# A hybrid attention layer: bias rows in key order, weight loads and norm steps put at other places of the program

## The chip, the core and the metric

One core of a Trainium2 chip runs the whole layer as one program. The metric is the device time of that program in microseconds; the median of three runs of the kernel before is 1379.38 us (1378.87 to 1380.16). Lower is better.

## What is computed

One encoder layer over 16 meta tokens and 1024 tokens of width 1024. After an RMS norm, one input projection yields the latents of group A (multi-head latent attention, 8 heads, dense), q, k and v of group B (neighbourhood attention, 16 heads of 64) and the gates of both groups. The core of group B:

```
s_win  = einsum(q_row, k_win) * scale + rel_bias[:, dr_idx, dc_idx]   # 8 rows x 16 columns of the 16 x 64 grid
s_meta = einsum(q_row, k_meta) * scale + meta_bias                    # 16 meta tokens: keys for every query
p      = softmax(concat(s_win, s_meta))
out    = p_win @ v_win + p_meta @ v_meta
```

Both groups' outputs are multiplied by SiLU of their gates, concatenated, projected by w_out and added to the input. Everything is float32; products are kept precise by splitting an operand into a high part (float32r) and a low part (the difference) and multiplying hi x hi, hi x lo and lo x hi.

## The kernel before

The stages, in the order of the program: (1) 0 to 83 us: the norm and the first two groups of gate columns. (2) 83 to 198 us: gate groups 2 to 5, each 384 columns (group 5: 128), as blocks of 128 columns by two halves of 512 tokens; one such gate is 24 matmuls. (3) 198 to 712 us: group B in 8 pairs of heads. (4) to 760 us: the latents. (5) to 1206 us: group A. (6) the output projection.

**Weights.** `w_split` (L139) loads a quarter of a weight block (two of the eight 128-row chunks) by a DMA on SP's queue into `wnf` (two buffers), ScalarE casts the high part `wnh`, and VectorE or GpSimd (`engs`) subtracts to get the low part `wnl`. `wnh` and `wnl` have six slots in pool `wp`; the last quarter (`own=wx`) has two slots `wnhx`, `wnlx` in a pool of its own, opened at L365 on memory which the setup used before.

**Bias.** In gate group 3, `bias_rows` (L377) makes 16 times two matmuls, and VectorE writes `base`, 24 column offsets by 16 key rows for each head. In groups 4 and 5, `stage_bias` (L390) has GpSimd lay out, for a pair of heads, three forms of the bias (800 values a partition for inner query tiles with the column mask added, 272 each for the first and the last tile) and sends them to `bias_d` in DRAM. `na_bias` (L454) loads the three forms of a pair.

**Group B's loop (L691).** Step g works on four query tiles at once: the projection of tile pr = g + 6 (t = pr mod 8 within pair p), scores `na_qk` of tile g + 1, transposes of the probabilities `na_ptr` of tile g, and probabilities times v `na_pv` of tile g - 1. TensorE's order is exactly the program's (`manual_schedule` for PE only); projections are cut into three parts with the other matmuls between them. All other engines' orders come from a planner, which places an instruction where its own model of the run finds its inputs and buffers ready and the engine free, and among several ready ones takes the one that stands earlier in the program. On the chip each engine then runs its list strictly in order. Parts of a step that the change touches: `na_load(p+1, t-2)` at the start of steps t = 2 to 5 (the weight splits of the next pair), `na_acc` (evictions of the projection: squares, raw q and k, `v_split`), `na_norm` in odd steps (sum, a power on GpSimd in `rstd` at L95, three small VectorE steps, one product), `na_meta` at t = 1 (16 matmuls for the meta tokens, at the end of the step, then their norm), `na_sum`/`na_fin` (reciprocals and gate product of four tiles) and `lat_nat` (the latents' norm, six tiles of it in the loop's last steps).

Of the kernel before, what the change touches and what calls it, by code (L numbers as in the profile page):

```python
# [10 lines left out]
F32 = mybir.dt.float32  # L11
F32R = mybir.dt.float32r
AF = mybir.ActivationFunctionType
ALU = mybir.AluOpType
# [20 lines left out]
WB = WI + 2 * WE  # L35
# [14 lines left out]
def hybrid_layer(ctx, tc, x, x_t, meta, meta_t, norm_w, w_na, w_g, w_lat, lat_w, w_uq, w_ukv, vec128, qpe_w, kpe_w,  # L50
# [27 lines left out]
    bias_d = dram.tile([NPAIR, P, 2, WB], F32, name="bias_d")  # L78
# [4 lines left out]

    def rstd(ss, n, cnt, np_=P, E=G):
# [3 lines left out]
        t = small.tile([P, n], F32, name="rs_t", tag=f"rs_t{n}")[:np_]  # L88

# [5 lines left out]
        G.tensor_tensor(y, v, mhalf[:np_, :n], op=ALU.pow)  # L95
        E.tensor_tensor(t, y, y, op=ALU.mult)
# [6 lines left out]
        return y  # L103

# [238 lines left out]
    base = sp1.tile([P, 16, NB, ROWS], F32, name="base")  # L343
# [40 lines left out]
    sg = sctx.enter_context(tc.tile_pool(name="stg", bufs=1))  # L384

    imask = load(c_imask, [P, WI], "imask", sp1)
    metab = load_bc(meta_bias, 16 * NM, "metab", sp1).rearrange("p (h m) -> p h m", h=16)
    G.tensor_scalar(metab, metab, -1.0, None, op0=ALU.mult)

    def stage_bias(p):  # L390

        E = G
        bs = base[:, 2 * p:2 * p + 2].rearrange("p h b r -> p h (b r)")
        bo = sg.tile([P, 2, WB], F32, name="sgb", bufs=3)
        bi, b0, b7 = bo[:, :, :WI], bo[:, :, WI:WI + WE], bo[:, :, WI + WE:]
        mb = metab[:, 2 * p:2 * p + 2, :]
        im = imask[:, None, :].to_broadcast([P, 2, WI])
        for o, bb, w in ((0, 0, 128), (144, 8, 128), (288, 16, 112)):
            E.tensor_tensor(bi[:, :, o:o + w], bs[:, :, bb * 16:bb * 16 + w], im[:, :, o:o + w], op=ALU.add)
        E.memset(bi[:, :, 128:144], MASK)  # L400
        E.tensor_copy(bi[:, :, 272:288], mb)
        for b_, c in ((b0, 128), (b7, 0)):
            E.tensor_copy(b_[:, :, 0:128], bs[:, :, c:c + 128])
            E.tensor_copy(b_[:, :, 128:144], mb)
            E.tensor_copy(b_[:, :, 144:272], bs[:, :, c + 128:c + 256])
        G.dma_start(bias_d[p], bo)

    todo_b = list(range(NPAIR))
    for gr in range(2, 6):
        gw = g_load(gr, (G, G) if gr < 4 else (V, V))  # L410
        for b in range(min(3, 16 - 3 * gr)):
            for hf in (1, 0):
# [6 lines left out]
                elif gr > 3 and todo_b:  # L419
                    stage_bias(todo_b.pop(0))  # L420
    sctx.close()
# [22 lines left out]
    st = {}  # L444

    def na_load(p, k):
        if k == 0:
            st[p] = {"w": []}
        d = st[p]
        d["w"].append(w_split(w_na[p, :, 2 * k:2 * k + 2, :], 384, (V, V), parts=True, own=wx if k == 3 else None))  # L450
        if k == 3:
            d["w"] = w_views(d["w"])

    def na_bias(p):  # L454
        c = 0
        for name, w, n in (("bi", WI, 2), ("b0", WE, 1), ("b7", WE, 1)):
            t = st[p][name] = np2.tile([P, 2, w], F32, name=name, bufs=n)
            nc.sync.dma_start(t, bias_d[p, :, :, c:c + w])
            c += w
# [7 lines left out]
    def na_nat(src, n, width):  # L467

        sq = np2.tile([P, 512], F32, name="sqn")[:n, :width]
        raw = np2.tile([P, P], F32, name="natm", bufs=1)[:n, :width]  # L470
        S.activation(sq, src, AF.Square)
        S.copy(raw, src)
        return na_norm(sq, raw, n, width)

    def na_norm(sq, raw, n, width):
# [3 lines left out]
        r = rstd(ss, g, 1.0 / 64, n, V)  # L479
        r3 = raw.rearrange("p (g d) -> p g d", g=g)  # L480
        V.tensor_tensor(r3, r3, r[:, :, None].to_broadcast([n, g, 64]), op=ALU.mult)
        return raw
# [17 lines left out]
    def na_meta(p):  # L500
        d = st[p]
        acc = bank("s")
        proj(acc[:, :256], NT, d["w"], 128, 384)
        kv = np2.tile([P, 256], F32, name="kvm", bufs=1)[:NM]
        meta_sum(kv, acc[:, :256])
        Vm = VM[p % 2]
        v_split(Vm, kv[:, 128:256], NM)
        d["Vm"] = Vm
        d["natm"] = na_nat(kv[:, :128], NM, 128)
# [7 lines left out]
    def na_acc(p, t, acc):  # L517
# [13 lines left out]
        d["V"][t] = vt  # L531

# [28 lines left out]
    def na_qk(p, t):  # L561
# [7 lines left out]
        for j in range(2):  # L569
# [7 lines left out]
                                   op0=ALU.add, op1=ALU.min, accum_out=mn)  # L577
            S.activation(sb, sb, AF.Exp, scale=-1.0, bias=mn, accum_out=d["sum", t // 4][:, t % 4, j:j + 1])  # L578
            d["p", t, j] = sb

    def na_ptr(p, t, j):

        d = st[p]
        sb = d["p", t, j]
# [44 lines left out]
    def na_sum(p, hf):  # L629
# [9 lines left out]
               r.rearrange("p t j -> p (t j)")[:, :, None].to_broadcast([P, 8, 64]))  # L639
        ps = bank("tr")  # L640
# [47 lines left out]
    for k in range(4):  # L688
        na_load(0, k)
# [625 lines left out]
```

## Time and profile before

| | us |
|---|---|
| median of three runs | 1379.38 |
| profiled execution | 1379.65 |
| its span in the profile | 1377.8 |
| TensorE busy | 1316.7 (96%) |
| VectorE busy | 958.1 (70%) |
| ScalarE busy | 809.8 (59%) |
| GpSimd busy | 436.4 (32%) |

The profiled execution is 1.85 us longer than its span, which begins with the first and ends with the last recorded instruction. A busy TensorE can run at either of two clocks, 1.2 or 2.4 GHz; the granted clock is given as a share of 2.4 GHz. "PE" is matmuls, "PEld" the loading of their weights, DVE is VectorE, ACT ScalarE, POOL GpSimd, SPq the queue on which SP issues DMAs.

### The profile page before, as it was taken

How to read it: one execution, taken by the hardware profiler on the slowest of the kernel's cores; microseconds unless marked ns; L12 is line 12 of the kernel's file. 1: busy time of each engine (PE TensorE's matmuls, PEld its weight loads, DVE VectorE, ACT ScalarE, POOL GpSimd, SP SyncE). 2: the span in 40 equal slices, each digit the busy share in tenths (PEclk: the TensorE clock that was granted, in tenths of full speed). 3: DMA queues.
4: the chain of work that ended last, by engine and by line, in shares of the span. 5: the costliest groups of instructions: out<-in, count | busy, mean ns of one | idle time of the engine just before them, and what ended most of it. 6: DMA issues, size and time to landing. Idle time of an engine off the chain costs nothing.

```text
span 1377.8 us, 24771 instructions
## 1 busy us (share of the span) xinstructions
PE 1316.7 (96%) x8116; PEld 1214.6 (88%) x8116; DVE 958.1 (70%) x3101; ACT 809.8 (59%) x2271; POOL 436.4 (32%) x936
## 2 busy tenths in 40 slices
PE   8989998999899999999889889999999999999998
PEld 7868888998898989889889889999999999988887
DVE  4924335887877888788768998987987988642110
ACT  6522124776767777777756667777777777630110
POOL 5330472121111211132344545734734652000000
PEclk9999999999999999999999999999999999999999
DMA  9352373222322222221111100100010022254231
GB/s 342 109 175 94 125 284 91 62 78 67 98 59 78 60 74 67 74 71 55 51 43 36 55 31 21 36 28 25 27 33 29 29 77 72 83 168 130 71 109 46
DMA packets 85694, 112.24 MB, mean 81 GB/s; under 512 B 10679, under 2 KB 63287, under 8 KB 85447
## 3 DMA queue, kind: packets, MB, share of 16 engines
q1 hardware_dynamic: 84415, 102.94, 24.1%
q0 software_dynamic: 1152, 7.73, 1.4%
q8 instruction: 64, 1.05, 0.3%
q14 instruction: 63, 0.52, 0.1%
HBM read 75.12 MB, written 29.23 MB: 76 GB/s over the span
## 4 chain that ended last, share of the span: by engine, by line
PE 69%; DVE 15%; ACT 4%; DMA 3%; issue 2%; POOL 1%; SPq 0%; DVEq 0%; ACTq 0%; POOLq 0%
PE ps_acc L109 21%; PE mps_acc L109 10%; PE ps_s L109 8%; PE mps_s L109 7%; PE mps_st L109 6%; PE mps_o L109 5%; PE ps_tr L112 4%; PE mps_tr L112 4%; PE ps_o L109 4%; DVE u_na L626 2%; DVE m_sb L988 1%; DVE PT L106 1%; DVE mPT L106 1%; ACT m_sb L997 1%; DMA Vp<-Vt 1%
## 5 line engine op out<-in xcount | busy, mean ns | idle before, releaser
L95 POOL TENSOR_TENSOR rs_y<-rs_v,mhalf 128x1 f32<-128x1 f32 (+5 forms) x170 | 148.2, 875 | 139.4 <-DVE rs_v L91 115.4
L109 PE MATMUL ps_acc<-wnh,hT 128*128 128x384 f32 (+1 forms) x432 | 163.3, 378 | 6.0 <-DVE Vt L106 4.5
L109 PE MATMUL ps_acc<-wnl,hT 128*128 128x384 f32 (+1 forms) x432 | 147.2, 341 | 0.0
L109 PE MATMUL ps_acc<-wnh,hTl 128*128 128x384 f32 (+1 forms) x432 | 147.1, 340 | 0.0
L547 POOL CAST qs<-qz 64x128 fp32r<-64x128 f32 x128 | 42.1, 329 | 298.3 <-ACT qz L543 281.2
L109 PE MATMUL mps_s<-mkT,mq 128*128 128x346 f32 (+1 forms) x576 | 132.1, 338 | 1.4 <-DVE mPT L106 1.0
L578 ACT ACTIVATE s_sb<-s_sb,nmn 128x400 f32<-128x400 f32 (+1 forms) x128 | 76.9, 601 | 61.2 <-DVE nmn L576 47.8
L109 PE MATMUL mps_o<-mPT,mV 128*128 128x256 f32 x768 | 106.2, 287 | 0.0
L1014 ACT CAST mPT<-mps_tr 128x512 fp32r<-128x512 f32 x128 | 74.4, 583 | 51.1 <-PE mps_tr L112 50.2
L988 DVE TENSOR_SCALAR_CACHE_REDUCE m_sb<-mps_s 128x346 f32<-128x346 f32 (+1 forms) x192 | 97.1, 512 | 9.0 <-PE mps_s L109 7.1
L106 DVE TENSOR_TENSOR mPT<-mps_tr,mPT 128x512 fp32r<-128x512 f32 x128 | 87.6, 685 | 13.3 <-ACT mPT L1014 12.1
L109 PEld LDWEIGHTS mps_s<-mkT,mq 128*128 128x128 f32 x576 | 93.3, 192 | 3.2 <-DVE mPT L106 1.6
L109 PEld LDWEIGHTS mps_o<-mPT,mV 128*128 128x128 f32 x768 | 94.9, 189 | 0.2
L109 PEld LDWEIGHTS ps_acc<-wnh,hT 128*128 128x128 f32 x432 | 84.7, 196 | 7.4 <-DVE Vt L106 4.8
L997 ACT ACTIVATE m_sb<-m_sb,mnm 128x1040 f32<-128x1040 f32 x64 | 74.6, 1166 | 23.2 <-DVE mnm L996 16.4
L109 PEld LDWEIGHTS ps_acc<-wnl,hT 128*128 128x128 f32 x432 | 84.6, 196 | 0.0
L109 PEld LDWEIGHTS ps_acc<-wnh,hTl 128*128 128x128 f32 x432 | 83.5, 193 | 0.0
L106 DVE TENSOR_TENSOR PT<-ps_tr,PT 128x384 fp32r<-128x384 f32 (+2 forms) x160 | 72.1, 467 | 12.7 <-ACT PT L599 11.8
L599 ACT CAST PT<-ps_tr 128x384 fp32r<-128x384 f32 (+2 forms) x160 | 62.0, 411 | 28.7 <-PE ps_tr L112 27.8
L112 PE MATMUL mps_tr<-ident,m_sb 128*128 128x128 f32 x512 | 76.7, 273 | 2.0 <-DVE mq L106 1.0
L109 PE MATMUL ps_o<-PT,Vt 128*128 128x256 f32 x256 | 60.5, 299 | 15.7 <-DVE PT L106 15.6
L106 DVE TENSOR_TENSOR kM<-ps_tr,kM 64x128 fp32r<-64x128 f32 x144 | 41.6, 289 | 34.8 <-ACT qz L543 30.1
(483 smaller groups left out, 3977.7 us busy)
## 6 DMA issues: line engine op xcount, KB each, us to landing
wnf<-in_w_na_dram SPq DMA_DIRECT2D x32, 384.0 KB, 3.3
g_d<-g SPq DMA_DIRECT2D x32, 256.0 KB, 2.7
wnf<-in_w_out_dram SPq DMA_DIRECT2D x32, 256.0 KB, 2.7
bias_d<-sgb POOLq DMA_DIRECT2D x8, 944.0 KB, 4.5
wnf<-in_w_g_dram SPq DMA_DIRECT2D x19, 384.0 KB, 6.5
Vp<-Vt SPq DMA_DIRECT2D x48, 112.0 KB, 2.2
yfo<-y_d SPq DMA_DIRECT2D x24, 192.0 KB, 2.8
b<-bias_d SPq DMA_DIRECT2D x16, 272.0 KB, 3.4
```

The source lines that it names most:

```text
L95: G.tensor_tensor(y, v, mhalf[:np_, :n], op=ALU.pow)
L106: eng.tensor_tensor(dst, src, f(hi), op=ALU.subtract)
L109: T.matmul(o, lhsT=l, rhs=r, start=start, stop=stop, skip_group_check=True)
L112: T.transpose(out=o, in_=i, identity=ident[: i.shape[0], : i.shape[0]])
L547: G.tensor_copy(qs[h_, j], qz[l_, j])
L578: S.activation(sb, sb, AF.Exp, scale=-1.0, bias=mn, accum_out=d["sum", t // 4][:, t % 4, j:j + 1])
L599: S.copy(pt[:n, c0:c1, 0, :], ps[:n, c0:c1])
L626: V.tensor_tensor(u[a], u[a], o[a], op=ALU.add)
L988: V.tensor_scalar(st["sb", h, t][:, ks], s_ps, -SCALE, BIG, op0=ALU.mult, op1=ALU.min, accum_out=st["mx", h, t][:, b:b + 1])
L997: S.activation(sb, sb, AF.Exp, scale=-1.0, bias=nm, accum_out=st["ms", h, t // 2][:, t % 2:t % 2 + 1])
L1014: S.copy(dh, ps)
```

## The change

`base` becomes one row of 432 keys for each head: three groups of 128 window keys followed by 16 meta keys (WB = 416 of it goes to DRAM). VectorE writes the window keys at their places directly, and the meta keys in two instructions. One DMA on SP's queue, after gate group 3, sends all heads; `stage_bias` and GpSimd's part go. In group B one DMA loads a pair's rows (`bs`); the first and last tile read slices of it; for the inner tiles VectorE adds the column mask once for a pair (`bi`, 128 x 800). Gate group 2 takes its fourth quarter from `wp` and not from `wx`; the low parts of groups 4 and 5 go to GpSimd. The first pair's weights stand in the program ahead of gate group 5, the later pairs' behind the evictions of their step. `rstd` is cut into two halves: sums and power, and in the next step the rest with the product. The meta tokens' norm is spread over steps t = 1 to 3, works in place (one copy fewer), and `na_sum` stands at the start of the step, its transposes at the end as before. The weights of the latents are loaded quarter by quarter in the last pair's steps, with VectorE for all low parts, and the latents' product comes one step later (`late`).

```diff
-WB = WI + 2 * WE
+WB = 416
-    bias_d = dram.tile([NPAIR, P, 2, WB], F32, name="bias_d")
+    bias_d = dram.tile([16, P, WB], F32, name="bias_d")
...
         G.tensor_tensor(y, v, mhalf[:np_, :n], op=ALU.pow)
+        return v, y
+
+    def rstd2(vy, n, np_=P, E=G):
+
+        v, y = vy
+        t = small.tile([P, n], F32, name="rs_t", tag=f"rs_t{n}")[:np_]
         E.tensor_tensor(t, y, y, op=ALU.mult)
...
-        return w_load(lambda k: w_g[:, 2 * k:2 * k + 2, gr * 384:gr * 384 + w], w, engs, wx)
+        return w_load(lambda k: w_g[:, 2 * k:2 * k + 2, gr * 384:gr * 384 + w], w, engs, wx if gr > 2 else None)
...
-    base = sp1.tile([P, 16, NB, ROWS], F32, name="base")
+    base = sp1.tile([P, 16, 432], F32, name="base")
+    basek = base.rearrange("p h (g c) -> p h g c", c=144)
...
-        V.tensor_scalar(base[:, :, :, rk], ps, -1.0, rmask[:, rk:rk + 1], op0=ALU.mult, op1=ALU.add)
+        V.tensor_scalar(basek[:, :, :, rk:128:16], ps.rearrange("p h (g b) -> p h g b", g=3), -1.0, rmask[:, rk:rk + 1],
+                        op0=ALU.mult, op1=ALU.add)
...
+    for k in range(2):
+        V.tensor_scalar(basek[:, :, k, 128:], metab, -1.0, None, op0=ALU.mult)
...
     for gr in range(2, 6):
-        gw = g_load(gr, (G, G) if gr < 4 else (V, V))
+        gw = g_load(gr)
+        if gr == 5:
+            for k in range(4):
+                na_load(0, k)
...
-                elif gr > 3 and todo_b:
-                    stage_bias(todo_b.pop(0))
-    sctx.close()
+        if gr == 3:
+            nc.sync.dma_start(bias_d.rearrange("h p n -> p h n"), base[:, :, :WB])
+            sctx.close()
...
+    def na_bias_load(p):
+        bs = st[p]["bs"] = np2.tile([P, 2, WB], F32, name="bs")
+        nc.sync.dma_start(bs, bias_d[2 * p:2 * p + 2].rearrange("h p n -> p h n"))
+        st[p].update(b0=bs[:, :, 144:], b7=bs[:, :, :WE])
     def na_bias(p):
...
+        bi = st[p]["bi"] = np2.tile([P, 2, WI], F32, name="bi", bufs=1)
+        V.tensor_tensor(bi, st[p]["bs"][:, :, :WI], imask[:, None, :].to_broadcast([P, 2, WI]), op=ALU.add)
...
+        acc = d["am"] = bank("s")[:, :256]
+        proj(acc, NT, d["w"], 128, 384)
+        kv = d["kvm"] = np2.tile([P, 256], F32, name="kvm", bufs=1)[:NM]
+        S.copy(kv, acc[32:MW])
+
+    def na_meta2(p):
+        d = st[p]
+        V.tensor_tensor(d["kvm"], d["am"][:NM], d["kvm"], op=ALU.add)
...
+    def na_meta4(p):
+        d = st[p]
+        na_norm2(d["vym"], d["kvm"][:, :P], NM, P)
+        d["natm"] = d["kvm"][:, :P]
...
-        if t % 2:
-            na_norm(sq, raw, P, 512)
-            d["nat"][t - 1], d["nat"][t] = raw[:, :256], raw[:, 256:]
         vt = np2.tile([P, 4, 64], F32R, name="Vt", bufs=8)
         v_split(vt, acc[:, 256:384], P)
         d["V"][t] = vt
+        if t % 2:
+            d["vy"] = na_norm1(sq, P, 512), raw
+
+    def na_acc2(p, t):
+        d = st[p]
+        vy, raw = d["vy"]
+        na_norm2(vy, raw, P, 512)
+        d["nat"][t - 1], d["nat"][t] = raw[:, :256], raw[:, 256:]
...
+        if late is not None:
+            late.append(lambda: lat_nat2(t, acc, nat, r))
+            return
...
-            if 1 < t < 6 and p + 1 < NPAIR:
-                na_load(p + 1, t - 2)
-            if t == 2 and p + 1 == NPAIR:
-                wk = w_load(lambda k: w_lat[:, 2 * k:2 * k + 2, 256:576], 320, (G, V))
...
         part(0, 1)
+        if late:
+            late.pop()()
+        if on(pr) and t == 2:
+            na_meta2(p)
+        if on(b - 1) and (b - 1) % 4 == 3:
+            na_sum((b - 1) // NT, (b - 1) % NT // 4)
         if on(b):
             na_pv(*divmod(b, NT))
+        if on(pr - 2) and pr % 2:
+            na_acc2(*divmod(pr - 2, NT))
         if on(a):
             na_ptr(*divmod(a, NT), 0)
...
+            if 1 < t < 6:
+                k = t - 2
+                if p + 1 < NPAIR:
+                    na_load(p + 1, k)
+                    if k == 3:
+                        na_bias_load(p + 1)
+                elif k < 3:
+                    wk.append(w_split(w_lat[:, 2 * k:2 * k + 2, 256:576], 320, (V, V)))
+            if pr == NSTEP - 1:
+                wk.append(w_split(w_lat[:, 6:8, 256:576], 320, (V, V)))
...
+        if a % NT == 7 and on(a + 1):
+            na_bias((a + 1) // NT)
         if on(b - 1) and (b - 1) % 4 == 3:
-            na_sum((b - 1) // NT, (b - 1) % NT // 4)
+            na_sum2((b - 1) // NT, (b - 1) % NT // 4)
...
+    im[:, 128:144] = MASK
```

## Rows read from the trace of the kernel before

**Rows 1.** The page's chain that ended last: share of the span by engine.

```profile
PE 69%; DVE 15%; ACT 4%; DMA 3%; issue 2%; POOL 1%; SPq 0%; DVEq 0%; ACTq 0%; POOLq 0%
```

**Rows 2.** Windows: start:end, us, busy PE PEld DVE ACT POOL, PEclk, DMA, GB/s.

```profile
208.00:217.00 9.00, 4.54 (x15) 4.54 (x16) 3.25 (x15) 1.93 (x8) 2.60 (x3) 0.62 0.89 276
255.00:262.00 7.00, 6.35 (x41) 6.21 (x42) 5.28 (x17) 4.55 (x14) 0.58 (x2) 1.00 0.26 77
262.00:324.00 62.00, 58.45 (x368) 55.75 (x366) 50.96 (x154) 45.63 (x138) 12.55 (x21) 0.97 0.25 72
311.80:324.80 13.00, 10.58 (x61) 9.82 (x60) 9.43 (x27) 7.74 (x25) 1.01 (x3) 0.87 0.30 93
```

**Rows 3.** Waits of matmuls, whole span: waiter <- releaser: total us, times, longest.

```profile
PE ps_o L109 <- DVE PT L106: 15.6, 13, 2.1
```

**Rows 4.** Timeline, PE, gate group 2: start, us, instruction [idle before <- releaser].

```profile
83.81 0.80 PE L109 MATMUL ps_acc<-hT,wnhx 128*128 128x512 f32 x1 [2.43 <-ACT wnhx L152]
...
86.77 0.52 PE L109 MATMUL ps_s<-hT,wnh 128*128 128x512 f32 x1
```

**Rows 5.** Chain in order of time, one undisturbed gate: start, us, what.

```profile
98.12 5.53 PE ps_s L109 x24
```

**Rows 6.** Timeline, ACT, casts of gate weights before and at the wait.

```profile
66.61 0.84 ACT L152 CAST wnh<-wnf 128x768 fp32r<-128x768 f32 x1 [1.86 <-DMA wnf<-in_w_g_dram]
...
82.93 1.56 ACT L152 CAST wnhx<-wnf 128x768 fp32r<-128x768 f32 x2 [1.64 <-DVE hM L106]
```

**Rows 7.** Timeline, PE, third step of group B, its 1st and 14th matmul.

```profile
212.46 0.69 PE L109 MATMUL ps_acc<-wnh,hT 128*128 128x384 f32 x1 [4.51 <-DVE Vt L106]
...
216.77 0.34 PE L109 MATMUL ps_acc<-wnl,hT 128*128 128x384 f32 x1
```

**Rows 8.** Timeline, SP's queue, ahead of that step: DMA issues.

```profile
207.19 1.26 SPq L143 DMA_DIRECT2D wnf<-in_w_na_dram  x2
208.51 0.85 SPq L69 DMA_DIRECT2D naw<-in_na_w_dram  x1
```

**Rows 9.** Timeline, DVE, ahead of that step.

```profile
211.98 0.16 DVE L431 SCALAR_TENSOR_TENSOR qkw_na<-naw 128x1 f32<-128x1 f32 x1 [3.88 <-DMA naw<-in_na_w_dram]
```

**Rows 10.** Timeline, PE, step t = 1 of pair 1: its longest wait.

```profile
255.65 0.38 PE L109 MATMUL ps_o<-PT,Vt 128*128 128x256 f32 x1 [1.47 <-DVE PT L106]
```

**Rows 11.** Timeline, PE, pair 2: steps t = 0 (305, 307) and t = 1.

```profile
305.28 0.28 PE L109 MATMUL ps_o<-PT,Vp 128*128 128x256 f32 x1
...
307.09 0.33 PE L109 MATMUL ps_acc<-wnl,hT 128*128 128x384 f32 x1
...
314.71 0.38 PE L109 MATMUL ps_o<-PT,Vt 128*128 128x256 f32 x1 [2.11 <-DVE PT L106]
...
315.64 0.54 PE L109 MATMUL ps_o<-PT,Vt 128*128 128x256 f32 x1 [0.31 <-DVE PT L106]
...
319.22 0.34 PE L109 MATMUL ps_acc<-wnl,hT 128*128 128x384 f32 x1
...
322.88 0.36 PE L109 MATMUL ps_s<-wnh,hM 128*48 128x256 f32 x1
```

**Rows 12.** Timeline, DVE, pair 2, step t = 1, just before that wait ends.

```profile
313.43 0.28 DVE L97 TENSOR_TENSOR rs_t<-rs_t,rs_v 128x8 f32<-128x8 f32 x1
313.64 0.55 DVE L106 TENSOR_TENSOR wnlx<-wnf,wnhx 128x384 fp32r<-128x384 f32 x1
```

**Rows 13.** Timeline, ACT: first casts of pair 3's weights.

```profile
300.47 1.75 ACT L150 CAST wnh<-wnf 128x384 fp32r<-128x384 f32 x4
```

**Rows 14.** Timeline, DVE: a product of two SBUF operands, 512 wide.

```profile
309.49 0.68 DVE L650 TENSOR_TENSOR gt<-gt,nrp 128x512 f32<-128x512 f32 x1
```

**Rows 15.** Timeline, DVE: weight splits with and without GpSimd's bias copies beside them.

```profile
182.90 3.55 DVE L106 TENSOR_TENSOR wnl<-wnf,wnh 128x384 fp32r<-128x384 f32 x4 [0.39 <-ACT wnh L150]
...
195.78 1.03 DVE L106 TENSOR_TENSOR wnl<-wnf,wnh 128x384 fp32r<-128x384 f32 x2 [1.49 <-ACT wnh L150]
```

**Rows 16.** Windows of the tile sgb alone: start:end, us, POOL busy, PEclk, DMA, GB/s.

```profile
156.00:195.00 39.00, 37.64 (x92) 1.00 0.62 233
```

More of the change, by code (lines that the diff above doesn't have):

```diff
@@ L103, in rstd @@
         return y
+    def rstd(ss, n, cnt, np_=P, E=G):
+        return rstd2(rstd1(ss, n, cnt, np_, E), n, np_, E)
     def lo_of(dst, src, hi, eng=V):
@@ L380, in bias_rows, with na_load @@
         mm(ps, selr[:, rk, :], rbl, False, True)
-        V.tensor_scalar(base[:, :, :, rk], ps, -1.0, rmask[:, rk:rk + 1], op0=ALU.mult, op1=ALU.add)
-    sg = sctx.enter_context(tc.tile_pool(name="stg", bufs=1))
-    imask = load(c_imask, [P, WI], "imask", sp1)
+        V.tensor_scalar(basek[:, :, :, rk:128:16], ps.rearrange("p h (g b) -> p h g b", g=3), -1.0, rmask[:, rk:rk + 1],
+                        op0=ALU.mult, op1=ALU.add)
     metab = load_bc(meta_bias, 16 * NM, "metab", sp1).rearrange("p (h m) -> p h m", h=16)
[L388 to L408, printed above, removed]
+    for k in range(2):
+        V.tensor_scalar(basek[:, :, k, 128:], metab, -1.0, None, op0=ALU.mult)
+    st = {}
+    def na_load(p, k):
+        if k == 0:
+            st[p] = {"w": []}
+        d = st[p]
+        d["w"].append(w_split(w_na[p, :, 2 * k:2 * k + 2, :], 384, (V, V), parts=True, own=wx if k == 3 else None))
+        if k == 3:
+            d["w"] = w_views(d["w"])
     for gr in range(2, 6):
-        gw = g_load(gr, (G, G) if gr < 4 else (V, V))
+        gw = g_load(gr)
+        if gr == 5:
+            for k in range(4):
+                na_load(0, k)
         for b in range(min(3, 16 - 3 * gr)):
@@ L443, in hybrid_layer @@
             G.memset(f(v[:, 2]), 0.0)
[L444 to L452, printed above, removed]
-    def na_bias(p):
[L455 to L459, printed above, removed]
+    imask = load(c_imask, [P, WI], "imask", np1)
+    def na_bias_load(p):
+        bs = st[p]["bs"] = np2.tile([P, 2, WB], F32, name="bs")
+        nc.sync.dma_start(bs, bias_d[2 * p:2 * p + 2].rearrange("h p n -> p h n"))
+        st[p].update(b0=bs[:, :, 144:], b7=bs[:, :, :WE])
+    def na_bias(p):
+        bi = st[p]["bi"] = np2.tile([P, 2, WI], F32, name="bi", bufs=1)
+        V.tensor_tensor(bi, st[p]["bs"][:, :, :WI], imask[:, None, :].to_broadcast([P, 2, WI]), op=ALU.add)
     def v_split(dst, src, n):
@@ L465, in v_split, with na_norm1 @@
         lo_of(dst[:n, 1:3, :], s2, dst[:n, 0:4:3, :])
[L467 to L475, printed above, removed]
+    def na_norm1(sq, n, width):
         g = width // 64
@@ L577, in na_qk @@
                                    op0=ALU.add, op1=ALU.min, accum_out=mn)
+            d["p", t, j] = sb, mn
+        for j in range(2):
+            sb, mn = d["p", t, j]
             S.activation(sb, sb, AF.Exp, scale=-1.0, bias=mn, accum_out=d["sum", t // 4][:, t % 4, j:j + 1])
-            d["p", t, j] = sb
     def na_ptr(p, t, j):
         d = st[p]
-        sb = d["p", t, j]
+        sb = d["p", t, j][0]
         ps = bank("tr")[:, :384].rearrange("p (c n) -> p c n", c=3)
@@ L659, in hybrid_layer, with lat_nat2, lat_nat @@
     order = [NT] + list(range(NT))
-    def lat_nat(t, acc, q, sq, pieces=None):
+    def lat_nat2(t, acc, nat, r):
+        V.tensor_scalar(nat[:, :256], acc[:, :256], r[:, 0:1], None, op0=ALU.mult)
+        V.tensor_scalar(nat[:, 256:], acc[:, 256:], r[:, 1:2], None, op0=ALU.mult)
+        nats["pe", t] = nat[:, 256:]
+        nats[False, t] = [nat[:, k_ * P:(k_ + 1) * P] for k_ in range(2)]
+    def lat_nat(t, acc, q, sq, pieces=None, late=None):
         n = P if t < NT else NM
@@ L687, in hybrid_layer @@
     NSTEP = NPAIR * NT
-    for k in range(4):
-        na_load(0, k)
+    na_bias_load(0)
     na_bias(0)
+    wk = []
+    late = []
     for g in range(-LEAD, NSTEP + 4):
```

53 lines of the change are left out of this document (31 added, 22 removed).

## The prediction

> **What bounds the kernel now.** I read the chain of waits first: its steps are matmuls for 69% of the span and VectorE for 15%, no other engine above 4% [rows 1]. TensorE's program is the same matmuls in the same order after the change, so time can come only from stretches in which it waits, or runs at 1.2 instead of 2.4 GHz after waiting. The windows show where those lie in group B: in a whole pair VectorE is busy 50.96 us of 62 beside TensorE's 58.45 [rows 2], the others have more room. The waits of matmuls then name the releaser: 15.6 us in 13 waits of `na_pv` for the low part of PT from VectorE, up to 2.1 us each [rows 3]. The reader is to see a kernel bound by TensorE, with VectorE so close behind that the order of its list decides.
>
> **The change, part by part.** All terms stand against the profiled execution's 1379.65 us; the median, 1379.38, is 0.02% below it.
>
> *Gate group 2's last quarter.* TensorE idles 2.43 us for `wnhx` [rows 4]. ScalarE could cast it only at 82.93, behind the subtraction for `hM` [rows 6], since `wx` lies on the setup's memory, while ordinary `wnh` casts for later groups ran at 66.61. From `wp` the quarter takes one of the slots that those casts use, so it is ready some 10 us before TensorE asks. After the idle, six matmuls take 86.77 - 83.81 = 2.96 us instead of 6/24 of 5.53 = 1.38 [rows 4, 5]: 1.58 at the lower clock. Together 2.43 + 1.58 = 4.0 us. In exchange group 3's third quarter waits for a slot of group 2; the slot frees after 6 of the 24 matmuls of group 2's last gate and the quarter is needed after 12 of the next one's, 30/24 of 5.53 = 6.9 us later [rows 5], in which a cast of 0.84 [rows 6] and two subtractions fit. Without that cover a wait like the one removed would stand one group later: bounds 0 and -4.0, I take -4.0.
>
> *Start of group B.* The third step waits 4.51 us [rows 7] for a low part of v, which sits in VectorE's list behind `qkw_na`, which waits for the tiny `naw` load [rows 9]. SP issued that load at 208.51, behind two weight loads two pairs ahead [rows 8]; it landed 3.4 us later. The granted clock of the stretch is 0.62 [rows 2]: 13 matmul intervals take 216.77 - 212.46 = 4.31 us, against 13 x 0.175 = 2.27 where a step is undisturbed (305.28 to 307.09 holds such matmuls) [rows 7, 11]. The stall is worth 4.51 + 2.04 = 6.55 us. The change takes two things out of this stretch: the last bias writes of GpSimd's queue, and two of the three bias loads of the first pair, while DMA engines are 0.89 busy [rows 2]. SP's two weight loads ahead of `naw` wait for buffers that earlier loads of this crowded stretch filled late, so I expect `naw` some 3 us earlier; the rest, 1.5 us, is like the 1.47 us wait in pair 1 [rows 10], whose window kept clock 1.00 [rows 2], so the clock loss goes too. -5.0 of bounds 0 and -6.55. That the first weights stand ahead of group 5 gives nothing by itself: no wait stands at the first step's matmuls.
>
> *Weight splits behind evictions, norms cut in two.* Step t = 1 of a pair waits 2.11 and 0.31 us for PT, and its matmuls then run slowly: from 315.64 to 319.22 they need 3.58 us, the same ones a step earlier 0.12 + (307.09 - 305.28) = 1.93, so 1.65 is clock [rows 11]; the window's clock is 0.87 [rows 2]. Five of the 13 waits of [rows 3] are of this kind, 61.5 us apart. Directly ahead of PT VectorE does a small step of the norm (0.21 to the next start) and a weight split (0.47), and a second split stands between the two PT halves [rows 12]. If these move behind, the first wait falls by 0.68 to 1.43, the second goes, and a 1.4 us wait costs no clock [rows 10]: 0.68 + 0.31 + 1.65 = 2.64 a pair, 13.2 in five. Against it: pair 3's casts begin at 300.47 [rows 13], although the program has them at t = 2 of pair 2, which begins only after the meta matmuls of 322.88 [rows 11]. The planner pulls them 20 us forward whenever slots are free; moving their place by one step need not matter. Only the norm's second half really loses rank against `na_pv`. Between 0 and -13.2 I take half, -6.6.
>
> *Mask added in the loop.* One VectorE instruction more for a pair, 128 x 800 of two SBUF operands. Not in the trace; 384 wide takes 0.55 and 512 wide 0.68 [rows 12, 14], which by its slope gives 0.68 + 288 x 0.00102 = about 0.98 us, an estimate. Seven of eight stand in the loop. VectorE has 11 us of a 62 us pair free [rows 2], but in pieces; where it hides, 0, where it stands ahead of PT, 7 x 0.98 = 6.9 plus clock. Nearest row: the split of 0.47 ahead of PT, which hides nothing. I take half, +3.4.
>
> At this place the rule that speaks against the change: four weight splits beside GpSimd's bias copies took 3.55 us, 0.89 each, two without them 1.03, 0.51 each [rows 15]. The Trainium skill, "GPSIMD Engine Reference", section Specifications, says that GpSimd shares its SBUF interfaces with VectorE and contends with VectorE instructions that have two SBUF inputs. The trace agrees. By it the mask sum, which is of that kind, would stretch by 0.89/0.51 when GpSimd works beside it, to 1.7 us, and the sum would be 2.5 us higher; without it, as above. GpSimd is busy 12.55 us of 62 in a pair [rows 2], so the sum goes without.
>
> *At nothing.* GpSimd's 37.64 us of layout copies [rows 16]: TensorE never waits for them. Its new subtractions for gate groups 4 and 5 are hidden by a group of 33 us; uncovered, a quarter would cost a wait like the 2.43 us of [rows 4]. The 16 `base` instructions keep their count and size; two small ones for the meta keys are new, beside gates. The one bias write of 3.3 MB takes some 15 us at the 233 GB/s of [rows 16], and gate results go out behind it on SP's queue; two g buffers and the PSUM banks before them hold three gates, 16.6 us [rows 5]. Without that room TensorE would wait the difference. One ScalarE copy a pair goes, hidden by 62 - 45.63 us of room [rows 2]. `na_sum`, the meta steps and `late` change ranks only: bounds of a wait each way, 1.5 us, taken as 0.
>
> **Sum**: -4.0 - 5.0 - 6.6 + 3.4 = -12.2; 1379.65 - 12.2 = 1367.4, so 1367 us.
>
> **Rivals.** *All short waits go*: with splits and norm steps out of VectorE's way the 5 clean pairs lose their whole stall, 2.11 + 0.31 + 1.65 = 4.07, and the start its whole 6.55: 1379.65 - 4.0 - 6.55 - 20.4 = 1348.7, about 1349. For it: the waits have one releaser [rows 3]. Against: the splits run early anyway [rows 13], and VectorE has more to do.
>
> *The change doesn't do what it says*: the planner pulls the splits to the same places and `naw` stays behind the weight loads; only the gate wait goes and the mask costs its half: 1379.65 - 4.0 + 3.4 = 1379.1, no change. For it: rows 13; against: fewer DMAs at 208 us.
>
> *Slower*: the mask sum of each of seven pairs is placed ahead of a PT half. VectorE has no slack there, the wait grows by 0.98 and TensorE falls to its lower clock for another 1.65 us, as at 314.71 [rows 11]: 7 x 2.63 = +18.4, with the first two terms kept 1379.65 - 9.0 + 18.4 = 1389.1. It decides from 9.0/7 = 1.3 us a pair on. For it: a split does just this today [rows 12]; against: the sum's inputs are there a whole step ahead, so it can lie where VectorE idles.
>
> **How the numbers follow.** The forecast has 0.47 (its own range 1357 to 1376), all short waits gone 0.20, no change 0.14, slower 0.19. A measurement here tells 0.2%, 2.8 us, from no change. Faster: 0.47 + 0.20 = 0.67; same 0.14; slower 0.19. The range reaches past the first rival, 1345, and to 1387, just under the third, which leaves about 0.08 and 0.10 outside.
>
> **What would show it.** Right: no wait at 83 us and granted clock 1.00 there; the third step of group B waiting under 2 us; in the windows of t = 1 a wait of PT of at most 1.5 us and no lower clock; pairs of about 60 us. Wrong: a longer wait for PT behind the mask sum; splits of pair p + 1 still ahead of PT at t = 1 with the 2.1 us wait unchanged; a new wait for a weight quarter at the start of gate group 3 or 5; gate results stuck behind the bias write at 160 to 175 us.

## The result, and the profile after

The changed kernel takes 1367.72 us (median of four runs, 1366.41 to 1368.06), the kernel before on the same chip 1379.77: a ratio of 0.991, 95% interval 0.9893 to 0.9927, so 10 to 15 us. Forecast: 1367. The profiled execution took 1367.42 us, its span 1365.6. The time agrees with the sum of the prediction; most of its terms do not, and this is what the rest is about.

Since TensorE's program is nearly the same, the two traces can be laid side by side at fixed matmuls. The table has the start of each in us:

| matmul | before | after | difference |
|---|---|---|---|
| first of group B | 197.58 | 191.71 | -5.87 |
| last meta product of pair 0 | 207.67 | 201.80 | -5.87 |
| of pair 1 | 263.18 | 250.55 | -12.63 |
| of pair 2 | 324.69 | 310.42 | -14.27 |
| of pair 7 | 630.03 | 614.99 | -15.04 |
| first scores of group A | 774.79 | 761.97 | -12.82 |
| first of the output projection | 1205.85 | 1193.78 | -12.07 |
| last | 1374.12 | 1362.05 | -12.07 |

So 5.87 us came in the gates, 6.76 at the start of group B, 1.64 in pair 2 and 0.77 in pairs 3 to 7 together; 2.22 went back ahead of group A and 0.75 in it.

**Chain and waits.** The chain of waits [rows 1] and the largest wait [rows 3] stand as before:

```profile
PE 71%; DVE 17%; ACT 5%; issue 3%; DMA 2%; POOL 1%; SPq 0%; ACTq 0%; POOLq 0%; DVEq 0%
```

```profile
PE ps_o L117 <- DVE PT L114: 15.9, 13, 2.1
```

The same stretches as in [rows 2], as windows of after (columns as there):

```profile
197.50:206.50 9.00, 9.00 (x59) 8.78 (x58) 4.80 (x12) 1.65 (x6) 2.73 (x5) 1.00 0.24 74
242.00:249.00 7.00, 5.97 (x38) 5.87 (x39) 5.47 (x17) 4.50 (x14) 0.58 (x2) 1.00 0.26 75
262.00:324.00 62.00, 58.52 (x375) 55.61 (x374) 53.28 (x159) 47.01 (x140) 12.61 (x21) 1.00 0.22 65
299.10:312.10 13.00, 10.58 (x74) 9.79 (x72) 10.64 (x32) 8.72 (x27) 2.52 (x4) 1.00 0.29 90
```

The start of group B has become a full 9.00 of 9 us at full clock; around step t = 1 of pair 2 TensorE is busy for the same 10.58 us of 13 as before, though for 74 matmuls and not 61.

**The gates.** TensorE has no wait over 0.15 us from 5.7 to 243 us. The quarter that was `wnhx` is cast early, as expected, and the 2.43 us of [rows 4] and the matmuls behind it at the lower clock are gone. But a second wait has gone too, which stands in the trace before and had no term in the sum:

```profile
76.99 0.50 PE L109 MATMUL ps_acc<-hT,wnh 128*128 128x512 f32 x1 [1.26 <-DVE g L257]
```

VectorE's list of before shows what made VectorE late there, and SP's queue of before who held that transfer up:

```profile
76.25 1.31 DVE L257 SCALAR_TENSOR_TENSOR g<-th,ps_acc 128x512 f32<-128x512 f32 x2 [6.41 <-DMA g_d<-g]
```

```profile
71.72 0.38 SPq L143 DMA_DIRECT2D wnf<-in_w_g_dram  x1
72.15 10.83 SPq L258 DMA_DIRECT2D g_d<-g  x7
```

The gate results waited on SP behind a weight load, and the load for a free `wnf` buffer. (The view merges seven stores into one line; the load held up the first two of them, which VectorE had made by 69.84 us and SP issued from 72.15 on.) In the trace after, on the same queue, the last loads come ahead of the results:

```profile
57.76 4.47 SPq L151 DMA_DIRECT2D wnf<-in_w_g_dram  x2
62.76 13.39 SPq L266 DMA_DIRECT2D g_d<-g  x8
```

At the matmuls themselves the trace after falls 0.27 us behind in the first 16 us, then gains 1.33 at the first wait, 2.60 at the second, 1.60 in the six matmuls behind it that ran at the lower clock, and 0.61 in those that follow. The first item is chance: at 16 us the other traces here stand between 2.07 us behind and 0.33 us ahead of before, with nearly the same program up to there. So the change is worth 6.14 us in the gates, and a difference of single traces carries this scatter.

**Start of group B.** SP's queue and VectorE's list after, to be read beside [rows 8, 9]:

```profile
196.33 0.33 SPq L151 DMA_DIRECT2D wnf<-in_w_na_dram  x1
196.71 0.47 SPq L69 DMA_DIRECT2D naw<-in_na_w_dram  x1
```

```profile
196.95 0.29 DVE L114 TENSOR_TENSOR Vt<-ps_acc,Vt 128x128 fp32r<-128x128 f32 x1 [0.65 <-ACT Vt L460]
200.03 0.16 DVE L432 SCALAR_TENSOR_TENSOR qkw_na<-naw 128x1 f32<-128x1 f32 x1 [2.79 <-DMA naw<-in_na_w_dram]
```

`naw` is still behind a weight load and VectorE still waits for it, 2.79 us. It costs nothing now: the low part of v that the third step of TensorE needs stands ahead of `qkw_na`, and even behind it that part would have been ready by about 200.5 (200.19 + 0.29). The third step begins at 201.92 with no wait.

**The loop.** Pair 2, step t = 1, and the same place in pair 3, on TensorE; then VectorE's list ahead of the first of them, which answers to [rows 11, 12]:

```profile
301.99 0.38 PE L117 MATMUL ps_o<-PT,Vt 128*128 128x256 f32 x1 [2.10 <-DVE PT L114]
302.92 0.39 PE L117 MATMUL ps_o<-PT,Vt 128*128 128x256 f32 x1 [0.31 <-DVE PT L114]
361.96 0.39 PE L117 MATMUL ps_o<-PT,Vt 128*128 128x256 f32 x1 [2.09 <-DVE PT L114]
```

```profile
300.71 0.28 DVE L101 TENSOR_TENSOR rs_t<-rs_t,rs_v 128x8 f32<-128x8 f32 x1
300.92 0.54 DVE L114 TENSOR_TENSOR wnlx<-wnf,wnhx 128x384 fp32r<-128x384 f32 x1
301.39 0.54 DVE L114 TENSOR_TENSOR PT<-ps_tr,PT 128x384 fp32r<-128x384 f32 x1
301.86 0.54 DVE L114 TENSOR_TENSOR wnlx<-wnf,wnhx 128x384 fp32r<-128x384 f32 x1
302.33 0.54 DVE L114 TENSOR_TENSOR PT<-ps_tr,PT 128x384 fp32r<-128x384 f32 x1
```

One split ahead of PT, one between the halves, the norm's small step ahead of both: as before, to the instruction. The waits are 2.10 and 0.31 us, against 2.11 and 0.31. What differs is the clock; windows of 8 us around the two waits, after:

```profile
300.99:308.99 8.00, 6.69 (x42) 6.38 (x43) 6.53 (x20) 4.45 (x14) 0.54 (x1) 1.00 0.45 134
360.96:368.96 8.00, 6.69 (x33) 6.45 (x34) 6.06 (x19) 3.44 (x11) 0.54 (x1) 0.79 0.46 134
```

With equal waits and equal busy time TensorE kept its clock in pair 2 and got 42 matmuls done instead of 33; in pairs 3 to 6 it fell, as it had in all five pairs before. That is the 1.64 us of pair 2.

It is no chance of one execution. In all five traces that have the changed loop with waits of 2.1 us (this one and those of the kernels below with the order undone, without the mask sum, with the latents' weights as before, and with one small tile more) pair 2 keeps its clock and takes 59.8 to 59.9 us; in all four traces with the loop of before (before, each early stall removed, both removed) it loses it and takes 61.1 to 61.5 us. In all nine the clock falls in pairs 3 to 6.

### The profile page after: what moved, and what is told of

Same layout as the page of the kernel before. It is cut to its first block, busy times and chain, and to the rows that moved or that the text cites. A ratio compares the mean times of both kernels' runs of the same rounds, so it can differ in the third digit from the quotient of the medians.

```text
span 1365.6 us, 24617 instructions
## 1 busy us (share of the span) xinstructions
PE 1312.9 (96%) x8116; PEld 1212.4 (89%) x8116; DVE 962.3 (70%) x3100; ACT 808.7 (59%) x2263; POOL 402.2 (29%) x851
## 4 chain that ended last, share of the span: by engine, by line
PE 71%; DVE 17%; ACT 5%; issue 3%; DMA 2%; POOL 1%; SPq 0%; ACTq 0%; POOLq 0%; DVEq 0%
PE ps_acc L117 20%; PE mps_acc L117 10%; PE ps_s L117 9%; PE mps_s L117 8%; PE mps_st L117 7%; PE mps_o L117 5%; PE ps_o L117 5%; PE mps_tr L120 4%; PE ps_tr L120 3%; DVE u_na L639 2%; DVE m_sb L1034 2%; DMA wnf<-in_w_na_dram 1%; DVE PT L114 1%; DVE qs L557 1%; ACT qz L554 1%
## 5 line engine op out<-in xcount | busy, mean ns | idle before, releaser
L114 POOL TENSOR_TENSOR wnl<-wnf,wnh 128x384 fp32r<-128x384 f32 (+2 forms) x62 | 53.0, 874 | 61.2 <-ACT wnh L160 55.0
```

What stands on the lines that cost most here:

```text
L114: eng.tensor_tensor(dst, src, f(hi), op=ALU.subtract)
```

## The experiments

Ratios are to the kernel before, measured beside each kernel on the same chip. Its medians were 1380.28 us (beside each early stall by itself, the order undone and the mask sum left out), 1378.31 (both stalls together, splits moved, product moved, latents as before), 1381.11 (pad, and the two kernels put together) and 1380.70 (the four small edits).

**Each early stall by itself, on the kernel before.**

```diff
-        return w_load(lambda k: w_g[:, 2 * k:2 * k + 2, gr * 384:gr * 384 + w], w, engs, wx)
+        return w_load(lambda k: w_g[:, 2 * k:2 * k + 2, gr * 384:gr * 384 + w], w, engs, wx if gr > 2 else None)
```

> The kernel before, with one edit: gate group 2 takes its fourth quarter from wp and not from wx. By the prediction's step the quarter is worth 4.0 us (the 2.43 us wait and 1.58 of lower clock): 1379.8 - 4.0 = 1375.8. By the theory from the trace after, the quarter also held up the queue: a later weight load waited on SP's queue for a wnf buffer, the gate results stood behind it, VectorE waited 6.41 us for a free g buffer, and TensorE 1.26 us for VectorE. Then both waits go and all 5.8 us that the two traces differ by at the start of gate group 2's second gate: 1374.0. Rival: it was another edit of the change that freed this stretch; then no wait at 83 us but the one at 77 us stays, or nothing changes: 1379.8 to 1377.

Measured 1372.66 us, 0.9946 (0.9933 to 0.9958). Both waits, at 77 and 83 us, are gone with this edit alone; the first matmul of group B starts 5.29 us earlier (6.14 if counted from 16 us on, as in the whole change), and the profiled execution ends 5.8 us earlier. The theory's 5.8 lies at the edge of the interval (5.8 to 9.2 us), the prediction's 4.0 outside. Part of the gain was taken back and returned later: the stall at the start of group B became longer,

```profile
208.22 0.69 PE L109 MATMUL ps_acc<-wnh,hT 128*128 128x384 f32 x1 [5.56 <-DVE Vt L106]
```

which was 4.51 us [rows 7].

```diff
+    naw = load(na_w, [P, 2], "naw")
     tabq_d = dram.tile([P, NT, 4, 32], F32, name="tabq_d")
...
-    naw = load(na_w, [P, 2], "naw", np1)
```

> The kernel before, with one edit: the small load of naw is issued at the start of the program (its tile lies in the pool const), its product qkw_na stays. Theory from the trace after: the third step of group B waits only because qkw_na stands in VectorE's list ahead of the low part of v and naw is issued on SP behind two weight loads; then this edit alone takes the whole 6.5 us, wait and clock: 1379.8 - 6.5 = 1373.3. Prediction's step: it takes 5.0 in the change because the stretch has fewer transfers, with 1.5 us of wait left. Rival: the crowded DMA engines and the late first weights set the start; then naw alone gives under 1.5 us and another wait takes its place: 1378.3 to 1379.8.

Measured 1370.24 us, 0.9931 (0.9918 to 0.9945). At pair 1 it stands 6.2 us ahead of before, 5.6 of them from the start of group B on: the small load was the stall, with the crowded stretch and GpSimd's bias writes left as they were. A wait of 0.99 us stays. The rival falls. The further 5 us of its profiled execution came far from `naw`: 2.5 in group A and 2.7 in the output projection, taken up below.

**Both together.**

> The kernel before with both small edits, nothing else: gate group 2's fourth quarter from wp, and naw loaded at the start of the program. Theory: these two stalls are all that the change removes; then this kernel has no wait at 77, 83 or 212 us, stands some 12 us ahead of the kernel before at the end of pair 0 of group B and ends within 2 us of the changed kernel (1367.7), a little better if the changed kernel's later waits (1.41 us at the first transposes of group A) don't come with these edits. Rival: bias rows, mask sum and order in the loop bring a share of their own; then this kernel ends 3 us or more behind the changed one. If the first t = 1 wait of 2.1 us, in pair 2, again costs no clock, the clock depends on what came before group B and not on the order in the loop.

Measured 1362.12 us, 0.9879 (0.9859 to 0.9898): two lines changed in the kernel before do at least as much as the changed kernel (0.991, 0.9893 to 0.9927). By the ratios that is some 4 us ahead of it, where within 2 was expected; the intervals just overlap. Pair 1 ends 11.90 us earlier than before, against 12.63 for the whole change. By the traces it is 2.15 us behind the changed kernel at the end of pair 7 and 5.72 ahead at the last matmul: 1.72 of this comes back in the latents, 3.45 in group A and 2.70 in the output projection. Its wait of 2.11 us in pair 2 did cost the clock (granted 0.79), so what spares pair 2 in the changed kernel is not the removal of the two stalls alone; nor is it the order in the loop, the mask sum or the latents' weights, since the kernels below that take these back keep the clock there. Which of the other parts does it stays open.

**The order in the loop undone.** In the changed kernel:

```diff
                 na_alloc(p)
+            if 1 < t < 6 and p + 1 < NPAIR:
+                na_load(p + 1, t - 2)
             acc = bank("acc")
...
             d["vy"] = na_norm1(sq, P, 512), raw
+            na_acc2(p, t)
...
-        if on(pr) and t == 2:
-            na_meta2(p)
...
                 na_meta(p)
+                na_meta2(p)
+                na_meta3(p)
+                na_meta4(p)
...
+            na_sum((b - 1) // NT, (b - 1) % NT // 4)
             na_sum2((b - 1) // NT, (b - 1) % NT // 4)
```

> The changed kernel with the loop's order undone: weight splits back at the start of their step, the second half of each norm directly behind the first, the meta norm in one piece at t = 1, na_sum in one piece at the step's end; mask sum, bias rows and everything before the loop stay as changed. Prediction's step: these moves are worth 6.6 us, so 1367.7 + 6.6 = 1374.3 (up to 1380.9 by its upper bound of 13.2). Theory from the trace after: the waits for PT at t = 1 are 2.10 and 0.31 us as before, since the planner puts the instructions where inputs and slots allow; undoing the moves gives 1367.7, within 0.5 us.

Measured 1367.23 us, 0.9907 (0.9893 to 0.9921). Waits at t = 1: 2.09 us and up to 2.12, as with the new order; pair 7 ends 0.2 us from the changed kernel. The engines' instruction lists say why: the two traces have the same list on each engine, instruction for instruction, but for the steps of the meta norm. The weight splits, the second halves of the 512-wide norms and `na_sum` stand at the same rank with either program. The term of 6.6 us is nothing.

**The mask sum left out.**

```diff
-        bi = st[p]["bi"] = np2.tile([P, 2, WI], F32, name="bi", bufs=1)
-        V.tensor_tensor(bi, st[p]["bs"][:, :, :WI], imask[:, None, :].to_broadcast([P, 2, WI]), op=ALU.add)
+        st[p]["bi"] = st[p]["bs"][:, :, :WI]
```

> The changed kernel without the mask sum: inner tiles read bs directly, so the column mask and the masking of the 16 meta places are left out, and with them eight VectorE instructions of 0.97 us and the load of imask. Prediction's step: half of seven stand in TensorE's way, 3.4 us: 1364.3. Upper bound of it: 6.9 us and more, 1360.8. Theory from the trace after: the sum runs near the end of step t = 2, where VectorE is some us ahead of TensorE; it is hidden: 1367.7, within 0.5 us.

Measured 1367.79 us, 0.9906 (0.9891 to 0.992): no difference. VectorE's list where the sum stands (in step t = 3, one later than the expectation has it), first with the sum (after), then without it:

```profile
322.43 0.97 DVE L455 TENSOR_TENSOR bi<-bs,imask 128x800 f32<-128x800 f32 x1
323.33 0.54 DVE L114 TENSOR_TENSOR PT<-ps_tr,PT 128x384 fp32r<-128x384 f32 x1
323.99 0.69 DVE L466 TENSOR_REDUCE ssn<-sqn 128x8 f32<-128x512 f32 x1
```

```profile
323.54 0.56 DVE L114 TENSOR_TENSOR PT<-ps_tr,PT 128x384 fp32r<-128x384 f32 x1 [0.38 <-ACT PT L610]
324.68 0.69 DVE L464 TENSOR_REDUCE ssn<-sqn 128x8 f32<-128x512 f32 x1 [0.58 <-ACT sqn L528]
```

Without the sum VectorE idles 0.38 + 0.58 = 0.96 us in its place, waiting for ScalarE. The estimate of 0.98 us was right (0.97); the sum lies in a gap of just its size. In the trace after all nine such instructions take 0.97 to 0.99 us; none is stretched to the 1.7 that the prediction gave for one beside GpSimd's work.

**What the loop's stall hangs on.** The changed kernel, with the fourth quarter's low parts on GpSimd, then with the product `gt` on GpSimd:

```diff
-        d["w"].append(w_split(w_na[p, :, 2 * k:2 * k + 2, :], 384, (V, V), parts=True, own=wx if k == 3 else None))
+        d["w"].append(w_split(w_na[p, :, 2 * k:2 * k + 2, :], 384, (G, G) if p and k == 3 else (V, V), parts=True, own=wx if k == 3 else None))
```

> The changed kernel with the low parts of the fourth weight quarter of each pair from pair 1 on (wnlx, two subtractions 128x384) on GpSimd and not on VectorE. One of them stands directly ahead of PT at t = 1 and one between the two PT halves. Prediction's step, if the splits had really moved: 0.47 less ahead of the first PT, the second wait of 0.31 us gone, and the clock loss of 1.65 us gone with a wait of about 1.6 us: 0.8 to 2.4 us a pair, five pairs: 1367.7 - 4 to - 12, about 1361. Rival: what holds PT is the chain through the transposes and ScalarE, or the clock falls all the same: 1367.7 - 4 at best.

```diff
-        V.tensor_tensor(gt, gt, rp, op=ALU.mult)
+        G.tensor_tensor(gt, gt, rp, op=ALU.mult)
```

> The changed kernel with one product of the output gating of group B (gt times the reciprocals, 128x512, 0.69 us, 16 of them) moved from VectorE to GpSimd. Theory: at t = 1 VectorE's list is full from the transposes on, so what stands in it decides the 2.10 us wait for PT; one 0.69 us product less shortens it to about 1.4 us in five pairs, and if TensorE then keeps its clock, another 1.65 us a pair: 1367.7 - 3.5 = 1364, or down to 1358. Rival: GpSimd's product comes later and the next step on VectorE waits for it with PT behind it: no gain, or up to 3 us lost.

The splits moved: 1360.63 us, 0.9861 (0.9843 to 0.988). The first wait is 1.77 us, the second gone, and the clock falls in three of five pairs instead of four. The wait fell by 0.33 and not by 0.47, mostly since one product on VectorE now runs beside GpSimd's splits (355.83 to 357.82 in this pair) and takes 0.94 us instead of 0.69:

```profile
357.42 0.94 DVE L669 SCALAR_TENSOR_TENSOR y_na<-y_na,gt 128x512 f32<-128x512 f32 x1
```

This is the contention that [rows 15] showed, now in the loop. The Trainium skill, "GPSIMD Engine Reference", Specifications, names the case, VectorE instructions with two inputs in SBUF, and the trace agrees. The product moved: 1362.14 us, 0.9867 (0.9846 to 0.9889); the wait is 1.39 us, but the clock still falls in four of five pairs, here in the second to fourth of them:

```profile
362.13:370.13 8.00, 6.36 (x30) 6.11 (x31) 6.76 (x20) 4.31 (x13) 0.96 (x2) 0.79 0.45 134
422.80:430.80 8.00, 6.36 (x40) 6.07 (x41) 7.10 (x20) 5.60 (x17) 0.96 (x2) 1.00 0.43 133
481.84:489.84 8.00, 6.36 (x30) 6.12 (x31) 6.76 (x20) 4.30 (x13) 0.96 (x2) 0.79 0.45 133
```

So a wait of 1.4 us does not spare the clock, as the prediction had read from the one in pair 1 [rows 10]. At the latents' start this kernel stands 3.7 us ahead of the changed one; 3.5 of them go again before group A, where a wait of 1.41 us has become 3.42. So the product stays on VectorE in the last pair below.

**What was given back.** The changed kernel, latents' weights and product as before:

```diff
+            if t == 2 and p + 1 == NPAIR:
+                wk = w_load(lambda k: w_lat[:, 2 * k:2 * k + 2, 256:576], 320, (G, V))
...
-                elif k < 3:
-                    wk.append(w_split(w_lat[:, 2 * k:2 * k + 2, 256:576], 320, (V, V)))
...
-            lat_nat(lt, acc, False, np2.tile([P, 512], F32, name="sqn")[:, :256], late=late)
+            lat_nat(lt, acc, False, np2.tile([P, 512], F32, name="sqn")[:, :256])
```

> The changed kernel with the weights of the latents as before (all four quarters at t = 2 of the last pair, low parts half on GpSimd, half on VectorE) and the latents' product in its own step. The two traces differ by 1.64 us at the first transposes of group A, where the changed kernel waits 1.41 us for mq from VectorE and runs at the lower clock, and by 0.65 us in a wait for kM in the last pair (2.42 against 1.77). Theory: both come with this part of the change: 1367.7 - 2 = 1365.7, no 1.41 us wait at the first mps_tr. Rival: they come from the shifted clock and the earlier start: 1367.7.

Measured 1364.03 us, 0.9893 (0.9874 to 0.9912), an interval that overlaps the changed kernel's. In the changed kernel, and in this one, at the first transposes of group A:

```profile
759.60 0.66 PE L120 MATMUL mps_tr<-ident,natl 128*128 128x128 f32 x2 [1.41 <-DVE mq L114]
```

```profile
757.93 0.64 PE L120 MATMUL mps_tr<-ident,natl 128*128 128x128 f32 x2
```

The wait is gone and the first scores of group A start 1.68 us earlier; the wait for `kM` in the last pair is 1.64 us, not 2.42. So by the traces this part of the change costs some 1.7 us; the run times do not tell it from nothing. `late` by itself leaves all lists of the engines as they are, so it is the weights' part that makes it.

**The output projection.** A tile of 128x1 more, called the pad below:

```diff
+    pad = const.tile([P, 1], F32, name="pad")
+    G.memset(pad, 0.0)
```

> The changed kernel with one more tile of 128x1 in the pool const and a memset of it at the start: every tile behind it on that side of SBUF lies 32 bytes further, nothing else changes. In the two runs with naw in that pool the output projection, from its first matmul with ymq on, took 165.6 us, in all others 168.3, with the same matmuls and the same granted clock of 1.00. Theory: the place of the tiles in SBUF makes this; then this kernel has 165.6 us in that stage too and 1367.7 - 2.7 = 1365.0 or some less. Rival: it was the early naw itself or chance: 168.3 us, 1367.7.

Measured 1363.79 us, 0.988 (0.9863 to 0.9897). From the first to the last matmul of the output projection it takes 165.56 us; the changed kernel takes 168.27. Windows of 120 us in this stage, first after, then with the pad:

```profile
1205.00:1325.00 120.00, 120.00 (x519) 97.21 (x518) 29.09 (x54) 19.56 (x40) 0.00 (x0) 1.00 0.37 117
```

```profile
1205.00:1325.00 120.00, 120.00 (x530) 99.11 (x529) 29.17 (x54) 19.54 (x40) 0.00 (x0) 1.00 0.37 117
```

530 matmuls instead of 519, with no wait and the clock granted in full. Group A, from its first scores to the first matmul of the output projection, did not get shorter with the pad (431.53 against 431.81 us), so the 2.5 us there in the run with the early `naw` is something else; this stage came out between 428.4 and 431.8 us over all runs, and why is open. With the tiles of the output projection at the same places the comparison of the two small edits with the whole change is 0.9879 to 0.988: the same.

**Put together.** The changed kernel with pad, splits on GpSimd and the latents' weights as before; then also `gt` on GpSimd in all pairs but the last:

> The changed kernel with three edits together: 32 bytes more in const, the fourth weight quarter's low parts on GpSimd, the latents' weights as before. If their gains add (2.7 from the output projection, some 6 to 8 from the loop, 2 to 3 from the latents): 1367.7 - 12 = 1356. If the mask sum, the bias rows and the splits on GpSimd leave VectorE's list at t = 1 the limit, and clock losses return elsewhere: 1360.

> The kernel of e11_best with, in addition, the product gt on GpSimd in all pairs but the last, where it cost 5.7 us at the latents. Theory: VectorE's list at t = 1 loses another 0.69 us ahead of PT, the first wait falls from 1.76 to about 1.1 us and TensorE keeps its clock in more pairs: 3 to 8 us below e11_best. Rival: GpSimd, which now holds splits, copies and the product, delivers late, and the wait for PT stays or another one comes up: the same as e11_best or above.

Measured 1352.60 us, 0.98 (0.9784 to 0.9816), and 1342.82 us, 0.9727 (0.971 to 0.9743). Both gained more than expected: the first is 3.4 us below 1356, of which group A gave 2.8 (429.03 against 431.81 us, open as above); the second is 9.8 us below the first, not 3 to 8. In the second, windows of 8 us around the five waits show the clock kept in four:

```profile
298.56:306.56 8.00, 6.91 (x45) 6.50 (x44) 6.61 (x21) 5.89 (x18) 0.97 (x2) 1.00 0.50 141
356.69:364.69 8.00, 6.90 (x44) 6.50 (x44) 6.62 (x21) 5.90 (x18) 0.96 (x2) 1.00 0.47 140
531.36:539.36 8.00, 6.90 (x33) 6.57 (x33) 6.67 (x20) 4.77 (x15) 0.97 (x2) 0.79 0.40 126
```

with waits of

```profile
357.69 0.39 PE L119 MATMUL ps_o<-PT,Vt 128*128 128x256 f32 x1 [0.93 <-DVE PT L116]
358.49 0.39 PE L119 MATMUL ps_o<-PT,Vt 128*128 128x256 f32 x1 [0.18 <-DVE PT L116]
```

An undisturbed pair takes 58.2 us there (307.81 to 365.98 between its meta products) against 61.4 (310.42 to 371.82) in the changed kernel.

**The four small edits on the kernel before** (quarter from `wp`, early `naw`, splits and, in all pairs but the last, `gt` on GpSimd):

> The kernel before with four small edits and none of the change's bias rows, mask sum or loop order: gate group 2's fourth quarter from wp, naw at the start of the program in the pool const, the fourth weight quarter's low parts and the product gt on GpSimd. Theory: the waits for PT at t = 1 hang on the number of instructions in VectorE's list ahead of it, not on the change's order, so this kernel has waits of about 0.9 us there, keeps TensorE's clock in the pairs and comes out as e12_gt does: a ratio to the kernel before of 0.973, within 0.002. Rival: the norm halves, the bias rows or GpSimd freed of the layout copies were needed for it: 0.980 or above.

Measured 1347.72 us, 0.9765 (0.9752 to 0.9778): the expectation of 0.973 within 0.002 missed. Waits at t = 1 are 0.92 us and the clock holds in all five pairs, so the loop is as expected, but the start of group B has a wait again, on TensorE and behind it on ScalarE:

```profile
205.30 0.44 PE L110 MATMUL ps_acc<-wnh,hT 128*128 128x384 f32 x1 [3.21 <-DVE Vt L107]
```

```profile
204.11 0.38 ACT L524 ACTIVATE sqn<-ps_acc 128x256 f32<-128x256 f32 x1 [6.74 <-POOL sgb L406]
```

ScalarE's first eviction of group B waits until GpSimd has copied the last bias forms, and GpSimd has a split of pair 1 ahead of them in its list, for which it waited itself:

```profile
197.03 1.02 POOL L107 TENSOR_TENSOR wnlx<-wnf,wnhx 128x384 fp32r<-128x384 f32 x1 [14.29 <-ACT wnhx L151]
```

With both small edits and no splits on GpSimd these copies end at 188.1 us, and ScalarE does not wait for them. The wait puts pair 1 3.5 us behind the kernel above; at the end of the profiled executions 1.8 of that are left. The ratios differ by 0.0038, 5 us; the rest is not in the traces, since the profiled execution is the fastest of five here (2.0 us below the median) and 1.0 us above the median there. So GpSimd's layout copies, which the change removes, do matter once GpSimd has splits to make as well.

## Why the prediction was right or wrong

The total was right, 1367 for 1367.7, and that is mostly luck: two terms were too small by 3.6 us together, and two others, of -3.2 together, were nothing:

| term | predicted | measured | by |
|---|---|---|---|
| gate group 2's quarter | -4.0 | -5.9 | traces; the edit alone 5.3 to 6.1 |
| start of group B | -5.0 | -6.8 | traces; `naw` alone 5.6, with 0.99 of wait left |
| splits and norms moved | -6.6 | 0 | loop order undone |
| mask sum | +3.4 | 0 | mask sum left out |
| clock in pair 2 | none | -1.6 | traces only, all five with this loop |
| pairs 3 to 7 | none | -0.8 | traces only |
| latents | 0 | +2.2 | traces; undone: 1.7 |
| after that | none | +0.8 | traces only |
| sum | -12.2 | -12.1 | |

**Gates.** The step was right in mechanism. Its term counted the wait and the clock behind it, and both were of the right size (2.60 and 1.60 us for 2.43 and 1.58); what it left out is the 1.3 us wait that comes from the results queued on SP behind a weight load, and the 0.6 us in the matmuls after the first six. The 1.26 us wait stood in the trace of before with VectorE as its releaser; one look at what VectorE waited for (6.41 us for `g_d`) leads to it.

**Start of group B.** The step said that `naw` comes some 3 us sooner and 1.5 us of wait stay. Issued at 196.71 instead of 208.51, against a stage that starts 5.87 us sooner, it came 5.9 us sooner in the stage, twice what the step took. Before, `qkw_na` ran 4.03 us after the time at which the third step would have begun without its wait (211.98 against 207.95); now it runs 1.9 us ahead of it. That alone ends the stall, and VectorE's new order, with the low part of v ahead of `qkw_na`, would have done so too. The whole stall went, so the 1.5 us that the step left standing is the part that was wrong. "The first weights ahead of group 5 give nothing by themselves" was not tried alone.

**Splits and norms.** This step failed, with the sign that the prediction had named for it: splits of the next pair still ahead of PT and the 2.1 us wait unchanged. The prediction gave the reason against it (the casts of pair 3 begin at 300.47, long before their place in the program, [rows 13]) and still took half, -6.6. The evidence in hand was for 0: a planner that takes the earliest ready instruction does not care about a place one step later. "Only the norm's second half really loses rank" was wrong too, its list is the same; only the meta norm's rank changed. The price of the stall, 2.64 us a pair, was of the right size, as the kernel with waits of 0.93 us shows (3.2 a pair); of its parts the clock's 1.65 was a little large, since the same matmuls took 2.04 us a step earlier (305.05 to 307.09), not 1.93, which makes it 1.54. But this clock part is not gone at the 1.4 us at which the prediction put it: waits of 2.1 us cost it in four or five pairs of five, 1.77 in three, 1.39 in four, 0.92 in one or none.

**Mask sum.** The duration was right, the place wrong. "The sum's inputs are there a whole step ahead, so it can lie where VectorE idles", the argument against the slower rival, was the one that held; it should have set the term.

**At nothing.** GpSimd's new gate subtractions, the `base` writes and the one bias write cost nothing: no wait of TensorE over 0.15 us up to 243 us. The latents' weights did.

**Rivals.** "The change doesn't do what it says" had the loop right and the start wrong; with the two early stalls at their whole size and the mask hidden it would have given 1379.65 - 5.9 - 6.8 = 1367. "All short waits go" needs the edits of the last kernels, not this change. "Slower" fell with the mask sum, which hides.

## What to carry to other kernels

Where a planner orders an engine, moving a line by one step is no change until the engine's instruction list differs: to take work out of the way of a stall, give it to another engine or have its inputs come later, and do not take half of the gain as a middle way. For a wait, follow the releaser back once more than the view does: a tiny load behind large ones on one queue cost here some 6 us, results behind a load that waits for a buffer 1.3 us, and one line each mended them. A forecast that comes out right can still be wrong in most of its terms; only the undoing of each part shows it.

## What the runs showed of the hardware that was not expected

The matmul rate depends on where tiles lie in SBUF. With every tile of one side 32 bytes further, the output projection runs 2% faster (530 against 519 matmuls in 120 us, both at granted clock 1.00); the stage takes 165.6 us in all six kernels whose tiles were shifted so and 168.3 in the other eight. Which operand's place matters no run here shows.

The clock fell or held after equal waits at the same place of the loop in different pairs of one execution (2.10 us: kept once, lost four times). With waits of 2.1 us it is always pair 2 that keeps it, in all five traces with the changed loop, and none of the five pairs in the four traces with the loop of before. What decides it beyond the wait's length, these runs do not show.
